# Attention in a decoder step: scores of head pairs in two double PSUM tiles, PE in source order

## The chip, the cores and the metric

The kernel runs on one core of a Trainium2 chip. The metric is the time of one execution on the device, in microseconds (us). The engines are called PE (TensorE, matmuls and transposes), DVE (VectorE), ACT (ScalarE), POOL (GpSimd) and SP (SyncE, which issues DMAs). PE writes its results into PSUM, eight banks of 512 f32 columns on 128 partitions.

## The reference

One inference step of a small hybrid decoder, width 1024, for a prompt of 256 tokens and 8 samples of one token each. Layer one is a state-space mixer (S5) and a squared-ReLU MLP; layer two is attention with three branches (compressed, selected and window keys), gated, and a second MLP. 16 query heads share 4 key and value heads of 64.

```python
kv = (_rms_norm(x, kv_norm) @ w_kv).reshape(nb, t, N_BRANCH, 2, N_KV_HEADS, HEAD_DIM)
# keys of the branches "selected" and "window": normed and rotated
k = _rope(_rms_norm(kv[:, :, br, 0], k_norm[br]), pos)
...
s_c = jnp.einsum('bqgrd,bngd->bqgrn', qg, kc)      # compressed: 8 blocks
p_c = _masked_softmax(s_c, ...)
s_s = ...; p_s = _masked_softmax(s_s, sel_mask)    # selected: here all 256 tokens
s_w = ...; p_w = _masked_softmax(s_w, w_mask)      # window: 256 tokens, causal
o = g[..., 0:1] * o_c + g[..., 1:2] * o_s + g[..., 2:3] * o_w
```

## The kernel before

All 264 tokens (8 samples, 256 prompt tokens) stand as columns, the width on the partitions. A dense layer takes 128x128 weight blocks; each weight is split into a high and a low part (`wh`, `wl`) and each block takes three matmuls of 264 columns (lines 597 to 599). The stages are S5, MLP, keys and values, queries and gates, attention, output projection, MLP. A scheduler of the language orders the instructions of each engine when the kernel is built; the source order is its input, and the pools of tiles (a tag has so many buffers) bind it, since a tile has to wait until its buffer is free.

Attention works on 12 units: two pairs of key heads (`gp`), two halves of the four query heads of each (`rp`), and for each the first 128 queries of two heads (`u` = 0) and then the last 128 of either (`u` = 1, 2). A unit has a step for the scores (`scores`), one for the softmax (`softmax`), one that turns the probabilities (`transposed`) and for `u` > 0 one that multiplies them with the values (`values`). The steps of three units run interleaved: scores of unit i, softmax of i-1, transposes and values of i-2. The two key heads of a pair (`g2`) lie in partitions 0 to 63 and 64 to 127; each has its own PSUM bank of scores, its own maximum, exponentials (with sums by ACT), reciprocal, gate and multiplication.

Around the units `side` calls two generators, `side_a` (the dense query tiles of the second head pair that are left, their norm and rotation in `q_post`, the compressed branch of the second half) and `side_b` (all of the samples' attention); tables say how many steps of each stand behind which unit:

```python
PSC = dict(fl=2, tr=3)
PSA = dict(mm=3)
PSB = dict(sc=2,po=1)
SIDE = (3,1,1,1,0,0,1,1,1,1,0,0,0,0)
SIDB = (1,2,2,2,2,2,2,2,0,0,0,0,0,0)
```

`PSC` are PSUM tags (banks each) that last the whole kernel, `PSA` those up to attention, `PSB` those from attention on. `kv_post` (lines 946 to 976) makes the keys ready: four transposes to token order (line 934, `token_major`), norm and rotation on ACT, DVE and POOL (`norm_rope`, lines 987 to 998), four transposes back (line 944, `feature_major`) and a copy into `KTp`, which the scores read. `q_post` does the same with two query heads, into `QT`. Two dense query tiles of the second pair stand ahead of attention (`Q1` = 2), two in `side_a`.

Of the kernel before, what the change touches and what calls it, by code (L numbers as in the profile page):

```python
# [157 lines left out]
def s5_stage(K, filler):  # L158
# [183 lines left out]
    def chunk_in(h):  # L342
# [3 lines left out]
        for q0 in range(0, 8, 3):  # L346
            n = min(3, 8 - q0)
            pt = [ps("mm"), ps("tr")]
# [177 lines left out]
    pys = {}  # L526
# [14 lines left out]
    for ft in range(4, 8):  # L541
        pys[ft] = ps("mm" if ft < 7 else "tr")
        conv(ft, pys[ft])
# [152 lines left out]
PDP = ()  # L696
PDA = ()
# [60 lines left out]
def sample_compress(K):  # L758
# [27 lines left out]
    for s in range(2):  # L786
# [3 lines left out]
        pts = [K.ps("fl"), K.ps("fl")]  # L790
# [157 lines left out]
def kv_post(K, br):  # L948
# [9 lines left out]
    pk = token_major(K, "sc", kv[:, 0:2])  # L958
# [6 lines left out]
    pv = token_major(K, "sc", kv[:, 2:4])  # L965
# [118 lines left out]
def gates(K, xh, xl):  # L1084
# [11 lines left out]
    S.activation(g, g, AF.Sigmoid)  # L1096
    K.gp = at.tile([128, 2, 16, 3], F32, name="gp")
# [44 lines left out]
def prompt_attn(K, oh, ol, side):  # L1142
# [6 lines left out]
    def cmp_branch(gp):  # L1149

        cS = aa.tile([128, 2, 8, 8], F32, tag="cS", name="cS", bufs=1)
        pcs = K.ps('po' if gp else PO)
# [22 lines left out]
        pt = K.ps('po' if gp else PO)  # L1175
# [3 lines left out]
        S.activation(pcts[gp], pt[0:64, 0:256], AF.Copy)  # L1179

    def scores(gp, rp, u):

        banks = [K.ps("sc"), K.ps("sc")]
# [16 lines left out]
        return banks  # L1200

    def softmax(gp, rp, u, banks):
        n = 4 if u == 0 else 2
        L = 512 // n
        out = []
        for g2 in range(2):
            head = (2 * gp + g2) * 4 + 2 * rp + max(u - 1, 0)
            sv = banks[g2].rearrange("p (n k) -> p n k", n=n)
            nm = aa.tile([128, n], F32, tag="nm", name="nm", bufs=6)
            den = aa.tile([128, n], F32, tag="den", name="den", bufs=6)  # L1210
# [5 lines left out]
            g = K.gp[:, 0, head:head + 2, 1:3] if u == 0 else K.gp[:, 1, head:head + 1, 1:3]  # L1216
            dv = den.rearrange("p (h b) -> p h b", b=2)
            V.tensor_tensor(dv, dv, g, ALU.mult)
            if (u > 0, g2) in PDA:
                for i in range(n):  # L1220
                    S.activation(P[:, i], P[:, i], AF.Copy, scale=den[:, i:i + 1])
            else:
                (G if (u > 0, g2) in PDP else V).tensor_tensor(P, P, den.unsqueeze(2).to_broadcast([128, n, L]), ALU.mult)
            out.append(P)
        return out

    def transposed(gp, rp, u, Ps, PTs):
        for g2 in range(2):
            pt = K.ps("tr")
            Pf = Ps[g2].rearrange("p n k -> p (n k)")  # L1230
# [29 lines left out]
    cmp_branch(0)  # L1260
    for i in range(n + 2):
        if i < n:
            sc[i] = scores(*units[i])
        if 1 <= i <= n:
            sm[i - 1] = softmax(*units[i - 1], sc.pop(i - 1))
        if i >= 2:
            gp, rp, u = units[i - 2]
            if u == 0:
                PTs = [aa.tile([128, 2, 2, 384], F32, tag="PT", name="PT", bufs=3) for _ in range(2)]
            transposed(gp, rp, u, sm.pop(i - 2), PTs)  # L1270
            if u > 0:
                values(gp, 2 * rp + u - 1, PTs[u - 1])
        side(i, cmp_branch)
# [17 lines left out]
def sample_qk(K):  # L1291
# [13 lines left out]
    if 1:  # L1305
        rsqrt_pool(nc, ak, ri, v, [128, 96])
    else:
        rsqrt_bits(nc, ak, ri, v, [128, 96])
    V.tensor_tensor(f(sq), f(K.sK), ri, ALU.mult)
# [14 lines left out]
    for gp in range(2):  # L1324
        for g2 in range(2):
            hs = slice(64 * g2, 64 * g2 + 64)
            c = 8 * gp + 4 * g2
            G.tensor_copy(K.Qbd[hs, :, gp, c:c + 4].rearrange("p b r -> p r b"), sR[hs, 4 + 4 * gp:8 + 4 * gp])

# [14 lines left out]
def sample_attn(K, oh, ol):  # L1344
# [6 lines left out]
    for bh in range(2):  # L1351
        p1, p2 = K.ps("mm"), K.ps("mm")
# [53 lines left out]
        pc = K.ps("mm")  # L1406
        nc.tensor.matmul(pc[:, 0:64], ptx[:, 0], K.vcs[:, bh], start=True, stop=True)
# [5 lines left out]
        V.tensor_tensor(o, o, pc[:, 0:64], ALU.add)  # L1413
# [34 lines left out]
def build(ctx, tc, A, O):  # L1448
# [13 lines left out]
    K.ps = lambda tag: pools[tag][0].tile([128, 512], F32, tag=pools[tag][2], name="ps_" + tag, bufs=pools[tag][1])  # L1462
# [63 lines left out]
    pools["mm"] = pools["fl"]  # L1526
    with ExitStack() as es:
# [59 lines left out]
        with ExitStack() as ek:  # L1587
            K.aa = ek.enter_context(tc.tile_pool(name="aa", bufs=1))

            def side_a(cmp_branch):  # L1590
                yield from q1
                for q in queue1:
                    yield from q
                cmp_branch(1)
                yield

            def side_b():
                sample_qk(K)
                yield
                yield from sample_attn(K, oh, ol)  # L1600
            steps = []

            def side(i, cmp_branch):
                if not steps:
                    steps.extend([side_a(cmp_branch), side_b()])
                for _ in range(SIDE[i]):
                    next(steps[0], None)
                for _ in range(SIDB[i]):
                    next(steps[1], None)
            prompt_attn(K, oh, ol, side)  # L1610
            for s in steps:
                for _ in s:
                    pass
        yh, yl = ft(F32R, "yh"), ft(F32R, "yl")
# [14 lines left out]
PSC = dict(fl=2, tr=3)  # L1629
PSA = dict(mm=3)  # L1630
PSB = dict(sc=2,po=1)
SIDE = (3,1,1,1,0,0,1,1,1,1,0,0,0,0)
SIDB = (1,2,2,2,2,2,2,2,0,0,0,0,0,0)
# [96 lines left out]
```

## Time and profile before

| | |
|---|---|
| median of 3 runs | 737.36 us (736.47 to 741.55) |
| the profiled execution | 741.12 us |
| its span, first to last instruction | 739.3 us |
| mean granted PE clock | 0.975 |
| PE busy | 700.2 us, 95% |
| DVE busy | 531.7 us, 72% |
| ACT busy | 404.6 us, 55% |
| POOL busy | 74.8 us, 10% |

The span is what the trace shows; the profiled execution's time has another 1.8 us around it. A mean granted clock of 1 would be PE at 2.4 GHz all the time. The attention stage, which the change is about, lies between some 435 and 528 us of the span.

### The profile page before, as it was taken

The numbers are of one execution on the slowest core, as the hardware profiler recorded it, in microseconds if no ns is written. First come the engines' busy times: TensorE is split into PE (matmuls) and PEld (weight loads), VectorE is DVE, ScalarE is ACT, GpSimd is POOL, SyncE is SP. The second block draws the span as 40 slices with busy tenths as digits, with TensorE's granted clock in tenths as the row PEclk, the third lists the DMA queues.
The fourth block names the chain that finished last, engine by engine and source line by source line (L and its number), as shares of the span: only waits on it lengthen the run. The fifth ranks groups of instructions, "written<-read, shape, count | busy, mean of one in ns | idle before, by whom it ended". The sixth has DMA issues, their size and how long they took to land.

```text
span 739.3 us, 16322 instructions
## 1 busy us (share of the span) xinstructions
PE 700.2 (95%) x6214; PEld 650.7 (88%) x6214; DVE 531.7 (72%) x1209; ACT 404.6 (55%) x907; POOL 74.8 (10%) x127
## 2 busy tenths in 40 slices
PE   2789897999999999999998999999999999999997
PEld 2787777999999999999988984565899999999997
DVE  7899995978777766656677868887678777755553
ACT  3463532666666655445466575657466666644442
POOL 0000623111000000000002224110020000000000
PEclk9989897999999999999999996999999999999999
DMA  7342423686767758555555564100255555556551
GB/s 263 81 158 77 161 99 118 197 289 193 229 234 262 277 175 298 186 175 188 177 175 179 188 187 142 59 3 1 86 172 182 188 173 182 189 180 201 192 190 40
DMA packets 53328, 124.70 MB, mean 169 GB/s; under 512 B 6522, under 2 KB 26874, under 8 KB 52994
## 3 DMA queue, kind: packets, MB, share of 16 engines
q1 hardware_dynamic: 51714, 121.23, 49.9%
q10 hardware_dynamic: 1536, 2.42, 0.9%
q8 instruction: 49, 0.80, 0.5%
q14 instruction: 29, 0.24, 0.1%
HBM read 120.63 MB, written 7.18 MB: 173 GB/s over the span
## 4 chain that ended last, share of the span: by engine, by line
PE 83%; DVE 13%; ACT 2%; issue 1%; DMA 1%; SPq 0%; ACTq 0%; DVEq 0%
PE ps_mm L597 23%; PE ps_mm L598 22%; PE ps_mm L599 22%; PE ps_sc L1195 3%; PE ps_tr L296 2%; PE ps_tr L1232 2%; PE ps_po L1253 2%; DVE ca L431 1%; DVE St L434 1%; DVE St L433 1%; DVE cb L432 1%; DVE St L455 1%; DMA U<-x_chunks_in 1%; DVE big L454 1%; PE ps_sc L1198 1%
## 5 line engine op out<-in xcount | busy, mean ns | idle before, releaser
L591 DVE TENSOR_TENSOR wl<-raw,wh 128x512 fp32r<-128x512 f32 x344 | 241.1, 703 | 149.5 <-ACT wh L590 146.5
L590 ACT ACTIVATE wh<-raw 128x512 fp32r<-128x512 f32 x344 | 216.0, 631 | 210.7 <-PE ps_mm L598 157.8
L597 PE MATMUL ps_mm<-hh,wh 128*128 128x264 f32 x512 | 145.3, 284 | 0.0
L598 PE MATMUL ps_mm<-hl,wh 128*128 128x264 f32 x512 | 145.0, 283 | 0.0
L599 PE MATMUL ps_mm<-hh,wl 128*128 128x264 f32 x512 | 145.0, 283 | 0.0
L598 PEld LDWEIGHTS ps_mm<-hl,wh 128*128 128x128 f32 x512 | 96.5, 188 | 0.0
L597 PEld LDWEIGHTS ps_mm<-hh,wh 128*128 128x128 f32 x512 | 96.4, 188 | 0.0
L599 PEld LDWEIGHTS ps_mm<-hh,wl 128*128 128x128 f32 x512 | 96.0, 187 | 0.0
L598 PE MATMUL ps_mm<-yl,wh 128*128 128x264 f32 x256 | 72.9, 285 | 0.0
L597 PE MATMUL ps_mm<-yh,wh 128*128 128x264 f32 x256 | 72.6, 284 | 0.0
L597 PE MATMUL ps_mm<-xh,wh 128*128 128x264 f32 x256 | 72.6, 284 | 0.0
L599 PE MATMUL ps_mm<-yh,wl 128*128 128x264 f32 x256 | 72.5, 283 | 0.0
L598 PE MATMUL ps_mm<-xl,wh 128*128 128x264 f32 x256 | 72.4, 283 | 0.0
L599 PE MATMUL ps_mm<-xh,wl 128*128 128x264 f32 x256 | 72.3, 284 | 0.0
L597 PEld LDWEIGHTS ps_mm<-yh,wh 128*128 128x128 f32 x256 | 48.2, 188 | 0.0
L598 PEld LDWEIGHTS ps_mm<-xl,wh 128*128 128x128 f32 x256 | 48.2, 188 | 0.0
L597 PEld LDWEIGHTS ps_mm<-xh,wh 128*128 128x128 f32 x256 | 48.2, 188 | 0.0
L599 PEld LDWEIGHTS ps_mm<-yh,wl 128*128 128x128 f32 x256 | 48.2, 188 | 0.0
L598 PEld LDWEIGHTS ps_mm<-yl,wh 128*128 128x128 f32 x256 | 48.1, 188 | 0.0
L599 PEld LDWEIGHTS ps_mm<-xh,wl 128*128 128x128 f32 x256 | 47.9, 188 | 0.0
L628 POOL TENSOR_TENSOR nacc<-nacc,sq 128x264 f32<-128x264 f32 x21 | 16.9, 803 | 251.9 <-ACT sq L627 251.9
L598 PE MATMUL ps_mm<-gl,wh 128*128 128x264 f32 x128 | 36.6, 289 | 0.0
(424 smaller groups left out, 1482.3 us busy)
## 6 DMA issues: line engine op xcount, KB each, us to landing
raw<-w_up_in SPq DMA_DIRECT2D x64, 512.0 KB, 3.8
raw<-w_down_in SPq DMA_DIRECT2D x64, 512.0 KB, 3.6
raw<-s_w_glu_in SPq DMA_DIRECT2D x16, 512.0 KB, 4.8
w<-cmp_w_in SPq DMA_DIRECT2D x12, 512.0 KB, 4.5
raw<-w_kv_in SPq DMA_DIRECT2D x12, 512.0 KB, 3.5
blk<-cache_cmp_in SPq DMA_DIRECT2D x64, 64.0 KB, 1.9
raw<-w_q_in SPq DMA_DIRECT2D x8, 512.0 KB, 3.7
win_old_out<-cache_win_kv_in SPq DMA_DIRECT2D x8, 510.0 KB, 5.2
```

Of the source, the lines that this page charges most:

```text
L296: nc.tensor.matmul(pm[:, 0:73], sameT, sq[:, h, q, b], start=(h + q + b == 0), stop=(h + q + b == 9))
L431: TT(a, x, m(SR), ALU.mult)
L432: TT(b_, x[:, ::-1], m(SQ), ALU.mult)
L590: nc.scalar.activation(h[:, :, cols], src[:, c:c + 4], AF.Copy)
L591: nc.vector.tensor_tensor(l[:, :, cols], src[:, c:c + 4], h[:, :, cols].bitcast(F32), ALU.subtract)
L597: nc.tensor.matmul(out, wh, xh, start=start, stop=False)
L598: nc.tensor.matmul(out, wh, xl, start=False, stop=False)
L599: nc.tensor.matmul(out, wl, xh, start=False, stop=stop)
L628: nc.gpsimd.tensor_tensor(self.acc, self.acc, sq, ALU.add)
L1195: nc.tensor.matmul(banks[g2], K.QT[hs[g2], 4 * gp + 2 * rp + u - 1, 128:256], K.KTp[hs[g2], gp], start=True, stop=False)
L1232: nc.tensor.transpose(pt[:, 128 * j:128 * j + 128], Pf[:, 128 * j:128 * j + 128], K.ident)
L1253: nc.tensor.matmul(po[64 * g2:64 * g2 + 64, 128 * kt:256], K.Vp[:, kt, br, 64 * g:64 * g + 64], rhs, start=False, stop=(br == 1 and kt == 1))
```

## The change

It has these parts. A tag `s2` of two tiles of two banks each takes the scores of a pair, and the two heads' score matmuls stand side by side. The softmax of a pair has one reduce, one reciprocal, one gate and one multiplication over 1024 columns; the exponentials stay one for each head and branch. PE is put in source order inside attention (`manual_schedule`), with a table that gives each step of side work a place between two units, ahead of the transposes (place 0) or behind them (place 1). Two dense query tiles are inside (`q` at units 0 and 1) and two ahead, as in the source before. Outside attention, dense work takes `fl` and the two `s2` tiles in turn; inside it takes `fl` alone. The keys' transposes move from `sc` to `tr`, which goes from three banks to two. `gates` loads the exponential's table early. `cmp_branch` and the samples' steps get yields, so that they can be cut.

```diff
     tm = K.ak.tile([128, 2, 512], F32, tag="tmk", name="tm", bufs=2)
-    pk = token_major(K, "sc", kv[:, 0:2])
+    pk = token_major(K, "tr", kv[:, 0:2])
...
     S.activation(g, g, AF.Sigmoid)
+    S.activation(ak.tile([1, 1], F32, name="tle"), g[0:1, 0:1], AF.Exp)
...
     def scores(gp, rp, u):

-        banks = [K.ps("sc"), K.ps("sc")]
+        pair = K.ps("s2")
+        banks = [pair[:, 0:512], pair[:, 512:1024]]
...
     def softmax(gp, rp, u, banks):
         n = 4 if u == 0 else 2
...
-        for g2 in range(2):
...
-            P = aa.tile([128, 522], F32, tag="P", name="P", bufs=4)[:, 0:512].rearrange("p (n k) -> p n k", n=n)
-            V.tensor_reduce(nm, sv, AX.X, ALU.max, negate=True)
-            for i in range(n):
-                S.activation(P[:, i], sv[:, i], AF.Exp, bias=nm[:, i:i + 1], accum_out=den[:, i:i + 1])
-            V.reciprocal(den, den)
...
+        sv = banks.rearrange("p (n k) -> p n k", n=2 * n)
...
+        P = aa.tile([128, 1024], F32, tag="P", name="P", bufs=2)
+        Pv = P.rearrange("p (n k) -> p n k", n=2 * n)
+        V.tensor_reduce(nm, sv, AX.X, ALU.max, negate=True)
+        for i in range(2 * n):
+            S.activation(Pv[:, i], sv[:, i], AF.Exp, bias=nm[:, i:i + 1], accum_out=den[:, i:i + 1])
+        V.reciprocal(den, den)
...
+        V.tensor_tensor(dv, dv, g, ALU.mult)
+        V.tensor_tensor(Pv, Pv, den.unsqueeze(2).to_broadcast([128, 2 * n, 512 // n]), ALU.mult)
+        return P[:, 0:512], P[:, 512:1024]
...
-    cmp_branch(0)
     for i in range(n + 2):
         if i < n:
             sc[i] = scores(*units[i])
         if 1 <= i <= n:
             sm[i - 1] = softmax(*units[i - 1], sc.pop(i - 1))
+        side(i, 0, cmp_branch)
         if i >= 2:
...
-        side(i, cmp_branch)
+        side(i, 1, cmp_branch)
...
-            prompt_attn(K, oh, ol, side)
-            for s in steps:
-                for _ in s:
+            K.mm = ["fl"]
+            with tc.manual_schedule(engines={nc.tensor.engine}):
+                prompt_attn(K, oh, ol, side)
+                for _ in steps["a"]:
                     pass
+            K.mm = list(wide)
...
-PSC = dict(fl=2, tr=3)
-PSA = dict(mm=3)
-PSB = dict(sc=2,po=1)
+PSC = dict(fl=1, tr=2)
+PSA = dict(mm=4, fb=1)
+PSB = dict(s2=2, po=1)
+SIDE = {(0, 0): "qc", (1, 0): "qc", (2, 0): "0", (3, 0): "0", (3, 1): "1s", (4, 1): "1", (5, 0): "s", (5, 1): "d",
...
```

Two places in PE's order. In such a row the line, the operation, output and inputs and their size stand, what it waits for, and how many like it follow one another (x4). Line numbers differ by a few between the two programs from the constants at 693 on: lines 932, 942, 1177, 1193, 1197, 1200 after are 934, 944, 1177, 1191, 1195, 1198 before.

The first is where the window keys, turned back (`tm`), come into the scores of unit 0. Before, on PE (`ps_mm`: the dense query tiles, which go on for another 20 rows until the scores L1191; the transposes of the same keys to token order stand 116 rows further up, most of the rows between dense):

```order
L597 MATMUL ps_mm<-qh,wh 128x264
L598 MATMUL ps_mm<-ql,wh 128x264
L599 MATMUL ps_mm<-qh,wl 128x264
L944 MATMUL ps_tr<-ident,tm 128x128 [waits Pool_49]
L944 MATMUL ps_tr<-ident,tm 128x128 x3
L1100 MATMUL ps_tr<-ident,gT 128x48 x2
L1108 MATMUL ps_tr<-cst,glt 128x3 [waits DVE_49,Activation_49]
L597 MATMUL ps_mm<-qh,wh 128x264
L598 MATMUL ps_mm<-ql,wh 128x264
L599 MATMUL ps_mm<-qh,wl 128x264
L1187 MATMUL ps_sc<-triR,identR 128x512
```

After, on PE, from those transposes (`kv`) to the scores (L1193) and the first dense row behind them:

```order
L932 MATMUL ps_tr<-ident,kv 128x128 [waits PE_49]
L932 MATMUL ps_tr<-ident,kv 128x128 x3
L1066 MATMUL ps_po<-ident,kcp 64x32 [waits DVE_49]
L1073 MATMUL ps_po<-vcp,cst 64x64 [waits PE_49,Activation_49]
L1073 MATMUL ps_po<-vcp,cst 64x64
L942 MATMUL ps_tr<-ident,tm 128x128 [waits Pool_49]
L942 MATMUL ps_tr<-ident,tm 128x128 x3
L932 MATMUL ps_tr<-ident,kv 128x128 x4
L1099 MATMUL ps_tr<-ident,gT 128x48 [waits Activation_49]
L1099 MATMUL ps_tr<-ident,gT 128x48
L1193 MATMUL ps_s_6037<-KTp,QT 128x256 x4
L597 MATMUL ps_fl<-qh,wh 128x264
```

The dense query tiles moved from between the two sets of transposes, and from ahead of the scores, to behind the scores.

The second is a query tile of the second half (`qr`, turned by L934 or L932), and the score matmuls of last queries. Before, on PE; the transposes back (L944 `qn`) follow 20 rows further down:

```order
L934 MATMUL ps_mm<-ident,qr_5939 128x128 [waits Activation_49]
L934 MATMUL ps_mm<-ident,qr_5939 128x128 x3
L1156 MATMUL ps_po<-kcb,QT 128x16 [waits DVE_49,PE_49]
L1156 MATMUL ps_po<-kcb,QT 128x16 x7
L1300 MATMUL ps_mm<-ssq,cst 128x96 [waits DMAHW4_49,DMAHW0_49,Activation_49]
L1195 MATMUL ps_sc<-KTp,QT 128x512 [waits DVE_49,Activation_49]
L1198 MATMUL ps_sc<-triR,identR 128x2x128
L1195 MATMUL ps_sc<-KTp,QT 128x512 [waits DVE_49,Activation_49]
L1198 MATMUL ps_sc<-triR,identR 128x2x128
L1195 MATMUL ps_sc<-KTp,QT 128x512 [waits DVE_49,Activation_49]
L1198 MATMUL ps_sc<-triR,identR 128x2x128
```

After, on PE, with the transposes of the compressed probabilities (`cS`) ahead, down to the transposes back (L942 `qn`):

```order
L1177 MATMUL ps_po<-ident,cS 64x128 [waits DMAHW3_49,DMAHW4_49,DVE_49,DMAHW7_49,PE_49,Pool_49]
L1177 MATMUL ps_po<-ident,cS 64x128
L1197 MATMUL ps_s_6165<-KTp,QT 128x512 [waits Activation_49]
L1197 MATMUL ps_s_6165<-KTp,QT 128x512
L1200 MATMUL ps_s_6165<-triR,identR 128x2x128 x2
L932 MATMUL ps_fl<-ident,qr_5941 128x128 [waits Activation_49]
L932 MATMUL ps_fl<-ident,qr_5941 128x128 x3
L1227 MATMUL ps_tr<-ident,P 128x128 x8
L1189 MATMUL ps_s_6229<-triR,identR 128x512 [waits PE_49]
L1189 MATMUL ps_s_6229<-triR,identR 128x512
L1193 MATMUL ps_s_6229<-KTp,QT 128x256 x4
L942 MATMUL ps_fl<-ident,qn 128x128 [waits Activation_49,Pool_49]
```

The two score matmuls became neighbours, and between the two sets of transposes of the query tile stand those of one unit (L1227) and the scores of one.

## Rows read from the trace of the kernel before

**Rows 1.** The page: busy us, share of the span and instructions by engine.

```profile
PE 700.2 (95%) x6214; PEld 650.7 (88%) x6214; DVE 531.7 (72%) x1209; ACT 404.6 (55%) x907; POOL 74.8 (10%) x127
```

**Rows 2.** Windows of the attention stage: length, busy us of each engine, clock, DMA share, GB/s.

```profile
core 0: us, PE busy (x) PEld busy (x) DVE busy (x) ACT busy (x) POOL busy (x), PEclk, DMA share, GB/s
441.00:446.00 5.00, 3.05 (x24) 2.66 (x23) 4.24 (x11) 4.83 (x16) 0.53 (x1) 1.00 0.88 257
446.00:460.00 14.00, 14.00 (x32) 6.91 (x31) 11.19 (x50) 7.15 (x28) 7.43 (x14) 0.51 0.42 136
...
500.00:521.00 21.00, 20.89 (x165) 11.84 (x157) 14.69 (x50) 12.86 (x56) 0.00 (x0) 1.00 0.00 1
```

**Rows 3.** Timeline of PE around its two waits: start, length us, operation, [idle before].

```profile
441.87 1.93 PE L1156 MATMUL ps_po<-kcb,QT 128*128 128x16 f32 x16 [0.35 <-DVE vcm L1079]
...
445.69 1.63 PE L1195 MATMUL ps_sc<-KTp,QT 64*128 64x512 f32 x2 [1.60 <-ACT P L1214]
...
447.75 2.07 PE L1195 MATMUL ps_sc<-KTp,QT 64*128 64x512 f32 x2
```

**Rows 4.** Timeline of PE: score matmuls of two row halves, together and one alone.

```profile
435.21 1.13 PE L1191 MATMUL ps_sc<-KTp,QT 64*128 64x256 f32 x8
...
476.31 1.13 PE L1191 MATMUL ps_sc<-KTp,QT 64*128 64x256 f32 x4
...
481.60 1.12 PE L1195 MATMUL ps_sc<-KTp,QT 64*128 64x512 f32 x2
```

**Rows 5.** Timelines of PE, DVE, POOL: the window keys, from transposes to transposes.

```profile
415.36 0.49 PE L934 MATMUL ps_sc<-ident,kv 128*128 128x128 f32 x3
...
417.52 0.67 DVE L988 TENSOR_REDUCE ss<-t 128x8 f32<-128x512 f32 x1
...
420.19 1.77 POOL L995 TENSOR_TENSOR tm<-tm,t 128x512 f32<-128x512 f32 x1 [2.62 <-ACT wh L590]
...
427.44 1.05 POOL L998 TENSOR_TENSOR tm<-tm,ri 128x512 f32<-128x512 f32 x1 [0.36 <-DVE ri L137]
...
430.65 0.60 PE L944 MATMUL ps_tr<-ident,tm 128*128 128x128 f32 x4
```

**Rows 6.** Timelines of ACT and DVE: the compressed keys and values handed on.

```profile
437.10 0.71 ACT L1070 ACTIVATE kcb<-ps_po 64x8 f32<-64x8 f32 x4 [1.31 <-PE ps_po L1068]
...
440.44 0.68 DVE L1079 TENSOR_TENSOR vcm<-ps_po,cst 64x512 f32<-64x512 f32 x1
```

**Rows 7.** Timelines of PE, ACT, POOL: a query tile of the second half, likewise.

```profile
474.66 0.60 PE L934 MATMUL ps_mm<-ident,qr 128*128 128x128 f32 x4
...
475.30 0.60 ACT L987 ACTIVATE t<-ps_mm 128x512 f32<-128x512 f32 x1 [0.18 <-PE ps_mm L934]
...
479.88 1.57 POOL L995 TENSOR_TENSOR qn<-qn,t 128x512 f32<-128x512 f32 x1 [12.62 <-ACT oh L606]
490.23 1.56 POOL L998 TENSOR_TENSOR qn<-qn,ri 128x512 f32<-128x512 f32 x1 [8.78 <-DVE den L1218]
...
491.84 0.66 PE L944 MATMUL ps_mm<-ident,qn 128*128 128x128 f32 x4
```

**Rows 8.** Timeline of ACT: exponentials of 256 and of 128 columns in a row.

```profile
474.08 0.49 ACT L1214 ACTIVATE P<-ps_sc,nm 128x256 f32<-128x256 f32 x1
...
474.53 0.49 ACT L1214 ACTIVATE P<-ps_sc,nm 128x256 f32<-128x256 f32 x1
...
479.64 0.36 ACT L1214 ACTIVATE P<-ps_sc,nm 128x128 f32<-128x128 f32 x1
...
479.99 0.37 ACT L1214 ACTIVATE P<-ps_sc,nm 128x128 f32<-128x128 f32 x1
```

**Rows 9.** Groups by shape, 441 to 530 us: count, busy us, mean ns, idle before.

```profile
L1223 DVE TENSOR_TENSOR P<-P,den 128x512 f32<-128x512 f32 x24 | 16.6, 691 | 0.4
...
L133 DVE TENSOR_TENSOR rs<-rs 128x8 f32<-128x8 f32 x6 | 1.3, 215 | 0.0
...
L606 ACT ACTIVATE oh<-ps_po 128x256 fp32r<-128x256 f32 x8 | 3.1, 384 | 10.4 <-PE ps_po L1253 10.0 <-PE ps_mm L1357 0.4
```

More of the change, by code (lines that the diff above doesn't have):

```diff
@@ L541, in s5_stage @@
     for ft in range(4, 8):
-        pys[ft] = ps("mm" if ft < 7 else "tr")
+        pys[ft] = ps("mm")
         conv(ft, pys[ft])
@@ L695 @@
 NP = 'm'
-PDP = ()
-PDA = ()
 CPA = (0,)
@@ L1151, in cmp_branch @@
         cS = aa.tile([128, 2, 8, 8], F32, tag="cS", name="cS", bufs=1)
-        pcs = K.ps('po' if gp else PO)
+        pcs = K.ps(PO)
         for qt in range(2):
@@ L1174, in cmp_branch @@
         V.tensor_tensor(cS, cS, dn.unsqueeze(3).to_broadcast([128, 2, 8, 8]), ALU.mult)
-        pt = K.ps('po' if gp else PO)
+        yield
+        pt = K.ps(PO)
         for qt in range(2):
@@ L1199, in scores @@
                                  K.triR.unsqueeze(1).to_broadcast([128, 2, 128]), start=False, stop=True)
-        return banks
+        return pair
     def softmax(gp, rp, u, banks):
         n = 4 if u == 0 else 2
-        L = 512 // n
-        out = []
-        for g2 in range(2):
[L1207 to L1210, printed above, removed]
-            P = aa.tile([128, 522], F32, tag="P", name="P", bufs=4)[:, 0:512].rearrange("p (n k) -> p n k", n=n)
-            V.tensor_reduce(nm, sv, AX.X, ALU.max, negate=True)
-            for i in range(n):
-                S.activation(P[:, i], sv[:, i], AF.Exp, bias=nm[:, i:i + 1], accum_out=den[:, i:i + 1])
-            V.reciprocal(den, den)
[L1216 to L1224, printed above, removed]
@@ L1351, in sample_attn @@
     for bh in range(2):
-        p1, p2 = K.ps("mm"), K.ps("mm")
+        pair = K.ps("s2")
+        p1, p2 = pair[:, 0:512], pair[:, 512:1024]
         for pp, o, n in ((p1, 0, 265), (p2, 265, 257)):
@@ L1405, in sample_attn @@
                                      vr[bh][br][:, b4, pg], start=False, stop=(br == 1 and pg == 1))
-        pc = K.ps("mm")
-        nc.tensor.matmul(pc[:, 0:64], ptx[:, 0], K.vcs[:, bh], start=True, stop=True)
+        pc = po[:, 256:320]
+        nc.tensor.matmul(pc, ptx[:, 0], K.vcs[:, bh], start=True, stop=True)
         t = K.tmp.tile([128, NT], F32, tag="t", name="so")[:, 0:256].rearrange("p (g d) -> p g d", g=4)
@@ L1412, in sample_attn @@
         V.tensor_reduce(o, t.rearrange("p g d -> p d g"), AX.X, ALU.add)
-        V.tensor_tensor(o, o, pc[:, 0:64], ALU.add)
+        V.tensor_tensor(o, o, pc, ALU.add)
         yield
@@ L1461, in psum, with ps @@
             pools[tag] = pool, bufs[tag], tag
-    K.ps = lambda tag: pools[tag][0].tile([128, 512], F32, tag=pools[tag][2], name="ps_" + tag, bufs=pools[tag][1])
+    K.mm = ["mm"]
+    def ps(tag):
+        if tag == "mm":
+            tag = K.mm[0]
+            K.mm.append(K.mm.pop(0))
+            if tag == "s2":
+                return ps(tag)[:, 0:512]
+        pool, bufs, t = pools[tag]
+        return pool.tile([128, 1024 if tag == "s2" else 512], F32, tag=t, name="ps_" + tag, bufs=bufs)
+    K.ps = ps
     psum(ctx, "pc", PSC)
@@ L1525, in build @@
     psum(ctx, "pa", PSB)
-    pools["mm"] = pools["fl"]
+    wide = ["fl", "s2", "s2"]
+    K.mm = list(wide)
     with ExitStack() as es:
@@ L1588, in build, with side @@
             K.aa = ek.enter_context(tc.tile_pool(name="aa", bufs=1))
[L1590 to L1609, printed above, removed]
-            prompt_attn(K, oh, ol, side)
-            for s in steps:
-                for _ in s:
+            steps = {"q": q1, "s": sample_qk(K), "a": sample_attn(K, oh, ol)}
+            def side(i, place, cmp_branch):
+                steps.setdefault("c", cmp_branch(0))
+                steps.setdefault("d", cmp_branch(1))
+                for x in SIDE.get((i, place), ""):
+                    next(steps[x] if x not in "01" else queue1[int(x)], None)
+            K.mm = ["fl"]
+            with tc.manual_schedule(engines={nc.tensor.engine}):
+                prompt_attn(K, oh, ol, side)
+                for _ in steps["a"]:
                     pass
+            K.mm = list(wide)
         yh, yl = ft(F32R, "yh"), ft(F32R, "yl")
```

21 lines of the change are left out of this document (14 added, 7 removed).

## The prediction

> **What bounds the kernel now.** The page comes first [rows 1]: PE is busy 700.2 of 739.3 us, DVE 531.7, ACT 404.6. So a microsecond that the change takes off DVE or ACT pays only where PE waits for it, and a wait that it puts before PE is paid in full. The windows of the attention stage say where PE waits today [rows 2]: 3.05 us of work in the five from 441 on, then no idle time worth naming up to 521 (14.00 of 14.00, and 20.89 of 21.00 at the end). The timeline names the two waits in the gap [rows 3]: 0.35 us for the masked compressed values, 1.60 us for a score bank that the first exponentials still hold. The third thing to see is the clock: the granted clock is 0.51 between 446 and 460, the lower of the two levels (1.2 of 2.4 GHz), right behind that gap, and 1.00 before and after. A 512-wide score matmul takes 2.07 us there [rows 3] and 1.12 later [rows 4]. The other engines wait for PE today, not PE for them: before the eight output splits ACT idles 10.0 us for PE's values [rows 9].
>
> The profiled execution took 741.12 us, 3.8 above the median of 737.36. I make the sum on the profiled one and take 3.8 off at the end.
>
> **What it can give.** Three terms.
>
> Scores in pairs. The heads of a pair lie in the two halves of PE's rows. Four 256-wide matmuls in both halves, issued in a row, take 1.13 us; the two of one bank alone take 1.13 as well [rows 4]. So neighbours in different halves run at the same time. Before, a 512-wide matmul (1.12 us) stands alone, with its mask and often transposes before its partner; after, the partners are neighbours. If the 512-wide ones overlap as the 256-wide do, each of 8 units saves 1.12 less a few hundredths for the start of the second, say 1.05: 8.4 us. Two of the four units of the first kind are split too (476.31 and its like): 2 x 1.05 = 2.1. Together 10.5; the lower bound is 2.1, if the wider ones don't overlap.
>
> The Trainium skill, "TensorEngine Tiling (Array Packing)", says that different row tiles must write different PSUM banks. The pair tile spans two banks, one for each head, so by that rule the 10.5 stands.
>
> The clock. At half clock 13.6 of the 14 us do 6.8 us of full-clock work. If nothing idles before it, 6.8 come back; the bound is 0.
>
> The waits of 0.35 and 1.60, with the table load that now sits in the gates: 2.0.
>
> DVE has half as many reduces, reciprocals and multiplications for the scores. A 512-wide one takes 0.69 [rows 9]; twice the width lies between 0.69 and 1.38 and I take 1.2, so 12 of each save some 4 us of DVE. None of it is PE's by itself, since PE waits for DVE nowhere between 446 and 521. ACT's exponentials are as many as before. The other tile sets before attention (one bank for side work, four for the dense work) move a few instructions under PE work that stays; I take 0, bounds -2 and +2.
>
> Gains: 10.5 + 6.8 + 2.0 = 19.3 us.
>
> **What it costs.** PE now runs the attention code in source order. What stands between a transpose and the matmul that needs its result is then fixed by hand, and where it is less than the chain, PE waits. For each such place I added the chain from rows and took off the PE work inside it; hand-overs between engines are counted at 0.2 each (0.18 in ACT's row of [rows 7]).
>
> First scores. The window keys were transposed at 415.36 and came back to PE at 430.65 [rows 5]: 15 us, all under dense matmuls. After, the transposes stand directly before the first scores, with small transposes alone between; the dense tiles that covered them stand behind those scores. The chain: square on ACT 0.6 (as at 475.30, rows 7), reduce, two products and scales on DVE 2.4 (0.67 for the first, rows 5), handing on the compressed keys 0.2 + 0.71 on ACT and the compressed values 1.28 on DVE, which is in DVE's order ahead of the end of the square root [rows 6], two small PE steps between, some 0.6 together (four transposes take 0.60, rows 7), the last four steps of the root 0.8 (0.2 each, rows 9), the multiplication on POOL 1.05, four transposes 0.45 and the copy 0.6, nine hand-overs 1.8, small transposes that share the two banks 1.5: 12.4, with 1.8 of PE work inside. **10.6.** Bounds: 8 (the root doesn't wait for the compressed values), 13 (the 15 us it took before, less the 1.8).
>
> Compressed probabilities of the first half. Their transposes stand ahead of the third scores. On DVE their normalising is queued behind the multiplication of the first pair, and that behind eight exponentials, 0.35 apart [rows 8]. **2.4**; bounds 0 and 4.
>
> First query tile of the second half. Before it took 17 us from 474.66 to 491.84 [rows 7], with thirty rows between. After, its two halves have eight transposes and one set of scores between them, 2.6 us. The chain: 0.6 on ACT, 2.4 on DVE (POOL's addition, 1.57, runs beside the root), six steps of the root 1.2, then in DVE's order the reduce of the scores just made (1.2) and the multiplication of the pair before (1.2 with 0.8 for its small ones), three more steps 0.6, POOL 1.3 to 1.56, hand-overs 0.6: 9.6 to 10. **7.0**; bounds 5 and 14 (17 less the 2.6).
>
> Second such tile, the same chain behind the eight exponentials of a unit and the output split: **4.7** where the sample's first small matmul stands ahead of it, and **2.6** at the sample's rotation, which is POOL's and DVE's. Bounds 3 and 14.
>
> Compressed probabilities of the second half: **3.9**, queued on DVE behind the reduce of the next pair. Bounds 1 and 6.
>
> The eighth scores, which wait for the exponentials of the unit two before, eight of 0.35 behind the sample's: **2.2**. Bounds 0 and 4.
>
> The rest: transposes of a unit and its values now stand together, with 0.6 us of PE work between a transpose and the copy that the values read (0.6 on ACT or DVE and two hand-overs), and two sample outputs wait for DVE's reduce: ten waits of 0.1 to 2.6, together **8.4**. Before, such neighbours had other units' scores between. Bounds 3 and 12.
>
> Losses: 10.6 + 2.4 + 7.0 + 4.7 + 2.6 + 3.9 + 2.2 + 8.4 = 41.8 us. Net 41.8 - 19.3 = 22.5 slower: 741.1 + 22.5 - 3.8 = 759.8. The bounds of the losses add up to 20 and 67, but DVE and ACT catch up in one wait what makes the next, so I don't expect both ends; I take 759.
>
> **The rivals.**
>
> The order holds (faster). PE waits at the first scores alone, and the engines have caught up in those 10.6 us, so that every later chain runs free: the two query tiles at their bare 0.6 + 2.4 + 2.2 + 1.3 less the work between are then some 3 us each, of which DVE's short queue takes another part. Losses 10.6 - 2.6 (its lower bound) = 8, and nothing else: 741.1 + 8 - 19.3 - 3.8 = 726. It decides if the waits add up to less than 12 us. For it: DVE loses 24 long instructions of 0.69 and gets 12 of 1.2. Against: the chains of rows 5 and 7 are latencies, not load, and no engine's idle time shortens them. 0.13.
>
> They cancel (no change, within 1%, about what a measurement of this kernel can tell from no change). The losses stay near their lower bounds, 20, and the gains are whole: 738. 0.15.
>
> The clock falls again. The lower level came in this trace after five microseconds with 3.05 busy [rows 2, 3]; the change makes at least one gap twice as long, and some shorter ones close together. Then the 6.8 is not won, and a second stretch of that length costs another 6.8: 759 + 6.8 to 759 + 13.6, 766 to 773; four of them 786. The Trainium skill, "TensorE: Matmul & The Clock Gate", section "A second HAM failure mode: psum-queue depth-cycling", speaks for this one: a kernel that cycles through PSUM banks with PE briefly idle between groups of matmuls sees its clock go up and down again. No row of the kernel before shows such a cycle, only the one fall. 0.25.
>
> The change doesn't do what it says: the 512-wide pairs run one after the other. 8.4 us of gain are gone, but a busier PE hides some 2.5 of the waits: 759 + 6 = 765. It lies inside the range; 0.1 within the forecast's own share.
>
> **How the numbers follow.** My forecast (745 to 766) has 0.47, the clock 0.25, no change 0.15, faster 0.13. Slower by over 1%: 0.47 + 0.25 = 0.72. The range leaves out most of the faster rival and four or more falls of the clock: 736 to 784.
>
> **What would show it.** In the profile after: no 512-wide score matmul alone, and two of them in about 1.2 us; PE idle for some 10 us before the first scores, released by ACT's copy of the keys or POOL's multiplication; 7 us before the second transposes of a query tile, released by POOL; sums of PE's idle time of 35 to 45 us between the first scores and the output projection; the clock low for at least one stretch. The forecast is wrong if the keys' transposes come earlier against the dense matmuls than the order of PE lets me see, if PE's idle time in the stage is under 20 us, or if time goes in the stages before attention, which I put at nothing.

## The result and the profile after

The changed kernel takes 766.04 us (762.80 to 770.64, 4 runs) against 739.45 (736.47 to 741.92, 4 runs) for the kernel before: 1.0366 times as long, 95% interval 1.0286 to 1.0446. The profiled execution took 763.48 us, its span is 761.7, its mean granted clock 0.966. The page, against [rows 1]:

```profile
PE 694.9 (91%) x6214; PEld 651.6 (86%) x6214; DVE 528.8 (69%) x1161; ACT 403.0 (53%) x908; POOL 70.1 (9%) x127
...
PEclk9979899999999999999999878999999999999999
```

PE is busy 5.3 us less and the span is 22.4 us longer: PE waits. The windows of the attention stage (length, busy us of each engine, clock, DMA share, GB/s), against [rows 2]:

```profile
core 0: us, PE busy (x) PEld busy (x) DVE busy (x) ACT busy (x) POOL busy (x), PEclk, DMA share, GB/s
425.00:445.00 20.00, 10.09 (x68) 8.47 (x69) 11.57 (x48) 8.94 (x22) 4.21 (x5) 0.71 0.12 40
445.00:470.00 25.00, 16.43 (x111) 12.84 (x107) 18.14 (x45) 12.48 (x48) 2.90 (x4) 0.91 0.28 96
470.00:500.00 30.00, 21.16 (x128) 14.04 (x132) 18.12 (x52) 12.22 (x45) 10.19 (x27) 0.84 0.20 63
500.00:530.00 30.00, 26.57 (x231) 15.96 (x224) 18.69 (x44) 18.01 (x80) 0.00 (x0) 0.97 0.24 72
530.00:560.00 30.00, 27.54 (x225) 21.90 (x226) 16.73 (x41) 14.53 (x46) 0.38 (x1) 1.00 0.13 42
```

In 75 us from 425 on PE works 47.7 (before, it had no idle time worth naming after 446), and the clock is between 0.71 and 0.91 in them. The waits of PE in the stage (us in total, times, longest):

```profile
engine line waited for: us in total, times, longest us
PE ps_fl L942 <- POOL qn L996: 7.0, 1, 7.0
PE ps_po L1066 <- DVE kcp L753: 4.0, 1, 4.0
PE ps_fl L1295 <- DVE rs L128: 4.0, 1, 4.0
PE ps_po L1177 <- DVE cS L1173: 3.7, 1, 3.7
PE ps_tr L942 <- POOL tm L996: 3.6, 1, 3.6
PE ps_fl L1414 <- DVE so L1411: 3.3, 2, 2.4
PE ps_po L1177 <- issue: 2.3, 1, 2.3
...
PE ps_tr L942 <- POOL qn L996: 1.3, 1, 1.3
```

These are the places of the prediction, one by one. At the first scores: 1.3 + 4.0 + 0.8 + 3.6 = 9.7 us, in this order for a query tile of the first pair on POOL (`qn`), the compressed keys (L1066, L1073) and the window keys on POOL (`tm`). Before the first query tile's transposes back: 7.0, for POOL. At the sample's first small matmul (L1295): 4.0. It writes the dense bank `ps_fl`, which the second query tile's norm reads until this row of DVE's timeline; the matmul starts at 480.69:

```profile
479.79 0.75 DVE L991 TENSOR_TENSOR t<-ps_fl,T1q 128x256 f32<-128x256 f32 x2
```

At the compressed probabilities: 2.3 and 3.7. PE's timeline shows the pair:

```profile
487.92 1.13 PE L1197 MATMUL ps_s<-KTp,QT 64*128 64x512 f32 x4
488.98 0.51 PE L1200 MATMUL ps_s<-triR,identR 128*128 128x256 f32 x2
```

Four records of 512 columns (two of each head) take 1.13 us, as two did before [rows 4]: the neighbours run at the same time. DVE's groups by shape (count, busy, mean ns, idle before) price the wide instructions, against 691 ns in [rows 9]:

```profile
L1219 DVE TENSOR_TENSOR P<-P,den 128x1024 f32<-128x1024 f32 x12 | 14.6, 1220 | 0.3
L1211 DVE TENSOR_REDUCE nm<-ps_s 128x4 f32<-128x1024 f32 x8 | 9.7, 1215 | 1.1 <-PE ps_s L1200 0.9
```

To compare the runs I take the stage from the first dense matmul of the keys (`kh`) to the first of the second MLP (`yh`), and split it for PE: gaps of over 0.1 us between its records (idle); half of the time that it is busy at the lower clock (what the clock costs); the rest is its work at full clock. The entries are good to 0.1. The idle time that the expectations below give for the changed kernel (33 us) leaves out 2.9 of it, two waits ahead of attention.

| kernel | ratio to before (95%) | stage us | idle | clock costs | work |
|---|---|---|---|---|---|
| before | 1 | 190.0 | 4.7 | 6.9 | 178.5 |
| changed | 1.0366 (1.0286 to 1.0446) | 214.7 | 36.1 | 10.2 | 168.5 |
| PE left to the scheduler | 1.0084 (1.0036 to 1.0132) | 196.8 | 19.2 | 6.9 | 170.8 |
| one transposes step later | 1.0259 (1.0161 to 1.0357) | 213.2 | 29.8 | 14.4 | 169.0 |
| four query tiles ahead | 1.0558 (1.0466 to 1.0650) | 230.9 | 39.3 | 23.1 | 168.5 |
| pairs taken apart | 1.0540 (1.0432 to 1.0649) | 230.2 | 31.7 | 21.5 | 177.1 |
| window keys first | 1.0330 (1.0252 to 1.0408) | 213.9 | 29.4 | 16.2 | 168.3 |
| waits filled with dummies | 1.0417 (1.0344 to 1.0490) | 216.5 | 27.0 | 10.2 | 179.3 |
| scheduler, softmax in halves | 1.0071 (0.9989 to 1.0153) | 194.8 | 16.9 | 7.8 | 170.2 |
| source order, wider table | 1.0266 (1.0170 to 1.0361) | 209.4 | 26.0 | 15.8 | 167.6 |
| scheduler, four single banks | 1.0223 (1.0119 to 1.0326) | 208.2 | 10.4 | 17.0 | 180.8 |
| source order, table moved again | 1.0157 (1.0040 to 1.0273) | 201.8 | 21.9 | 11.0 | 168.9 |
| scheduler, halves, keys first | 1.0036 (0.9985 to 1.0088) | 194.2 | 14.8 | 10.7 | 168.7 |
| the same with the wider table | 1.0007 (0.9958 to 1.0057) | 190.6 | 12.7 | 8.3 | 169.6 |

What stands ahead of the stage (354.8 to 363.9 us) varies from execution to execution, and what stands behind it takes 190 us in all of them; neither goes with the change. So the stage's 24.7 us are the loss: 31.4 more idle, 3.3 more for the clock, 10.0 less work.

The split is of one execution of each kernel, and executions of the same kernel differ in their granted clock. The profiled one of the changed kernel has the highest of its four (0.966; the others 0.964, 0.958 and 0.955, with times up to 770.64), so the 3.3 is probably the low end of what the clock takes there. A difference in the clock column says something about an edit only where the other executions bear it out. They do for four tiles ahead (0.943 to 0.947 in all four) and pairs taken apart (0.941 to 0.952) against the changed kernel (0.955 to 0.966), and for four single banks (0.955 to 0.963) against the scheduler with halves (0.968 to 0.977). They don't for one transposes step later, window keys first and source order with the wider table, whose mean clocks (0.964, 0.959 and 0.961) lie within 0.004 of the changed kernel's 0.961.

### The profile page after: what moved, and what is told of

The parts are those of the page before. It is cut to its first block, busy times and chain, and to the rows that moved or that the text cites. A ratio compares the mean times of both kernels' runs of the same rounds, so it can differ in the third digit from the quotient of the medians.

```text
span 761.7 us, 16256 instructions
## 1 busy us (share of the span) xinstructions
PE 694.9 (91%) x6214; PEld 651.6 (86%) x6214; DVE 528.8 (69%) x1161; ACT 403.0 (53%) x908; POOL 70.1 (9%) x127
## 4 chain that ended last, share of the span: by engine, by line
PE 76%; DVE 14%; ACT 5%; issue 2%; DMA 1%; POOL 1%; SPq 0%; ACTq 0%; DVEq 0%; POOLq 0%
PE ps_mm L598 10%; PE ps_mm L597 10%; PE ps_mm L599 10%; PE ps_s L598 8%; PE ps_s L597 8%; PE ps_s L599 8%; PE ps_fl L597 4%; PE ps_fl L598 4%; PE ps_fl L599 4%; ACT P L1213 2%; PE ps_tr L296 2%; DVE P L1219 1%; PE ps_fl L793 1%; PE ps_fb L793 1%; PE ps_po L1248 1%
## 5 line engine op out<-in xcount | busy, mean ns | idle before, releaser
L597 PE MATMUL ps_mm<-hh,wh 128*128 128x264 f32 x256 | 72.6, 284 | 0.0
L598 PE MATMUL ps_mm<-hl,wh 128*128 128x264 f32 x256 | 72.5, 283 | 0.0
L599 PE MATMUL ps_mm<-hh,wl 128*128 128x264 f32 x256 | 72.5, 283 | 0.0
L597 PE MATMUL ps_s<-hh,wh 128*128 128x264 f32 x192 | 54.5, 284 | 0.0
L598 PE MATMUL ps_s<-hl,wh 128*128 128x264 f32 x192 | 54.4, 283 | 0.0
L599 PE MATMUL ps_s<-hh,wl 128*128 128x264 f32 x192 | 54.4, 283 | 0.0
L598 PEld LDWEIGHTS ps_mm<-hl,wh 128*128 128x128 f32 x256 | 48.2, 188 | 0.0
L597 PEld LDWEIGHTS ps_mm<-hh,wh 128*128 128x128 f32 x256 | 48.2, 188 | 0.0
L599 PEld LDWEIGHTS ps_mm<-hh,wl 128*128 128x128 f32 x256 | 48.0, 187 | 0.0
L597 PE MATMUL ps_s<-yh,wh 128*128 128x264 f32 x168 | 47.7, 284 | 0.0
L628 POOL TENSOR_TENSOR nacc<-nacc,sq 128x264 f32<-128x264 f32 x21 | 16.2, 773 | 255.7 <-ACT sq L627 255.6
```

The source lines that it names most:

```text
L597: nc.tensor.matmul(out, wh, xh, start=start, stop=False)
L598: nc.tensor.matmul(out, wh, xl, start=False, stop=False)
L599: nc.tensor.matmul(out, wl, xh, start=False, stop=stop)
L628: nc.gpsimd.tensor_tensor(self.acc, self.acc, sq, ALU.add)
```

## Experiments

The theory: PE's fixed order leaves chains of other engines uncovered, and the neighbouring pairs pay back some 10 us. The rivals: what costs is the bank layout with the wide softmax; or it is the clock.

**PE left to the scheduler.** All else as changed.

```diff
-            with tc.manual_schedule(engines={nc.tensor.engine}):
+            if True:
                 prompt_attn(K, oh, ol, side)
```

> The changed kernel with PE in attention left to the scheduler again (all else as changed: pair tiles, single softmax instructions, banks, table of side work). Theory (fixed order of PE leaves the chains uncovered): PE's idle time in the stage falls from 33 us to under 10, the dense query tiles lie between the two sets of key transposes again, time 733 to 745 us. Rival (the bank layout and the wide softmax cost it: one dense bank, two transpose banks, two buffers of probabilities): idle stays over 25 us, 758 to 768.

749.21 us, stage 196.8: 17.9 of the 24.7 us are gone, 16.9 of them idle. Its largest waits:

```profile
PE ps_s L1197 <- ACT P L1213: 3.8, 2, 3.5
PE ps_fl L1309 <- DVE ssq L1307: 2.4, 1, 2.4
...
PE ps_fl L942 <- DVE sv L1297: 1.6, 1, 1.6
```

The 7.0, the 4.0 and 3.6 for the keys, and both waits for compressed probabilities are no more; the largest that is left is for a score tile that the first exponentials hold. The theory holds for most of the loss, though not for all: idle is 19.2, not under 10, and the time lies above the range. The share of the wide softmax and of the score tiles is what later runs ask; the other banks (one for dense work, two for transposes) weren't varied in any run.

**One transposes step later.** One entry of the table.

```diff
-SIDE = {(0, 0): "qc", (1, 0): "qc", (2, 0): "0", (3, 0): "0", (3, 1): "1s", (4, 1): "1", ...
+SIDE = {(0, 0): "qc", (1, 0): "qc", (2, 0): "0", (3, 1): "1s", (4, 0): "0", (4, 1): "1", ...
```

> The changed kernel with one entry of the table moved: the transposes back of the first query tile of the second half stand one unit later. Theory (the wait is the chain less the PE work inside): the 7.0 us wait before them goes to under 1.5; the chain of the second tile now ends nearer, so its waits (4.0 and 0.35) grow by 1 to 3; net -3 to -6 us, 760 to 763. Rival (POOL or DVE is too slow at this place whatever PE's order): the wait moves along with the transposes and stays over 5 us, time as the changed kernel.

761.50 us, as forecast, though its interval overlaps the changed kernel's. The largest waits:

```profile
PE ps_fl L1295 <- DVE rs L128: 4.6, 1, 4.6
PE ps_po L1066 <- DVE kcp L753: 4.0, 1, 4.0
PE ps_po L1177 <- DVE cS L1173: 3.7, 1, 3.7
PE ps_tr L942 <- POOL tm L996: 3.6, 1, 3.6
```

The wait of 7.0 is gone and hasn't moved along, so it was the place, not POOL. The next one grew by 0.6, and a new one of 1.1 came before values; idle fell by 6.3. In the profiled execution the stage gained only 1.5, as the clock took 4.2 of it (10.2 to 14.4) and work 0.5. That isn't the edit's doing as far as the runs show: the profiled execution is the slowest of its four (764.20), and their mean clock is no lower than the changed kernel's (0.964 against 0.961).

**Four query tiles ahead.** The two dense tiles inside attention go to the front.

```diff
-SIDE = {(0, 0): "qc", (1, 0): "qc", ...
+SIDE = {(0, 0): "c", (1, 0): "c", ...
-Q1 = 2
+Q1 = 4
```

> The changed kernel with all four dense query tiles of the second pair ahead of attention instead of two inside. Theory: the scheduler puts them between the two sets of key transposes, the 9.7 us idle before the first scores (4.0 + 0.8 + 3.6 + 1.3) falls under 2.5; 5.8 us of cover are then missing behind the first scores, so that new waits of 3 to 6 us come before the compressed probabilities' or the first probabilities' transposes; net -3 to -6 us, 759 to 763. Rival (the cover isn't what is missing): the idle before the first scores stays over 7 us.

782.54 us, which neither the theory nor the rival had. The two largest waits in PE's timeline, and the window that holds them:

```profile
448.10 1.11 PE L942 MATMUL ps_tr<-ident,tm 128*128 128x128 f32 x4 [5.79 <-POOL tm L996]
...
469.31 0.61 PE L1177 MATMUL ps_po<-ident,cS 128*64 128x128 f32 x2 [9.41 <-issue]
```

```profile
445.00:470.00 25.00, 12.49 (x50) 9.17 (x50) 9.39 (x27) 7.38 (x33) 1.65 (x2) 0.50 0.16 58
```

The scheduler did put the dense tiles between the keys' transposes, and the idle time there fell from 9.7 to 6.6, not under 2.5: 5.8 us of cover against a chain that the prediction put at 12 and that took 11.2 in the changed kernel (from the end of the keys' transposes, 432.41, to the first scores, 443.65). Then 9.4 us open where the tiles had stood, before the compressed probabilities. The clock is 0.50 all through the window and costs 23.1 us in the stage, 12.9 more than in the changed kernel. With the dense tiles gone from attention, more went to the clock than to waits; I had priced only the waits.

**Pairs taken apart.** Each score matmul followed by its own mask.

```diff
             for g2 in range(2):
                 nc.tensor.matmul(banks[g2], K.QT[hs[g2], 4 * gp + 2 * rp + u - 1, 128:256],
                                  K.KTp[hs[g2], gp], start=True, stop=False)
-            for g2 in range(2):
                 nc.tensor.matmul(banks[g2].rearrange("p (b k) -> p b k", b=2)[:, :, 128:256], K.identR,
```

> The changed kernel with each 512-wide score matmul followed at once by its own mask, so that the partners in the two row halves are no neighbours. Theory (neighbours overlap): a pair with its masks takes 1.05 us more, 8.4 us of PE work in 8 units, of which 2 to 4 lie in waits that exist already: +4 to +7 us, 770 to 773. Rival (512-wide ones don't overlap): no difference in PE's busy time, time as the changed kernel.

781.76 us, above the range. The score matmuls as a group, in the changed kernel and here, and two windows of this run:

```profile
L1197 PE MATMUL ps_s<-KTp,QT 64*128 64x512 f32 x32 | 9.8, 690 | 0.0
```

```profile
L1197 PE MATMUL ps_s<-KTp,QT 64*128 64x512 f32 x32 | 20.9, 739 | 0.0
```

```profile
445.00:470.00 25.00, 22.09 (x101) 16.59 (x101) 10.87 (x28) 10.77 (x39) 2.36 (x3) 0.70 0.21 67
470.00:500.00 30.00, 19.77 (x80) 13.00 (x81) 18.15 (x50) 10.84 (x41) 8.72 (x16) 0.67 0.27 87
```

Busy time of the group doubles, work rises by 8.6 us (8.4 forecast) and idle falls by 4.4, as the theory has it. The time rose by more than it allows, because the clock costs 11.3 more. That taking the pairs apart brings the lower clock is shown by this edit (all four executions lie below all four of the changed kernel); by which mechanism isn't.

**Window keys first.** One constant.

```diff
-KVQ = 0
+KVQ = 1
```

> The changed kernel with the window keys' dense tiles ahead of the first queries' (one constant), so that the keys' chain has the four dense query tiles of the first pair to run under; the first query tile's transposes now stand 46 dense matmuls (5.6 us) ahead of its transposes back. Theory (a chain of 10 to 12 us less the PE work put inside it): of the 9.7 us idle before the first scores some 4 to 5 are left (10 less 5.6, now for the queries), the rest of the stage as in the changed kernel; -4 to -8 us, 757 to 762. Rival (the first scores wait for something else than the keys): idle there stays over 8 us, time as the changed kernel.

764.35 us, above the range. Of the 9.7 us idle before the first scores 4.8 are left, as forecast, but not for the queries: they are the 4.0 and 0.8 of the compressed keys, which stayed as they were, a chain of its own that I had not priced apart. (The queries' came behind the scores, 1.2 and 0.7.) Idle in the stage fell by 6.7. In the profiled execution the clock took 6.0 of it; over the four executions the mean clock is 0.959 against 0.961 and the interval overlaps the changed kernel's, so what the edit is worth in time stays open.

**Waits filled with dummies.** Six places of the table's waits (the expectation counts seven), 88 transposes of the identity in all.

```diff
+def fill(K, out, n):
+
+    for _ in range(n):
+        K.nc.tensor.transpose(out, K.ident, K.ident)
...
         pt = K.ps(PO)
+        fill(K, pt[:, 256:384], 24 if gp else 12)
```

> The changed kernel with dummy transposes of the identity put on PE in seven of its waits (4 to 24 of about 0.11 us, into parts of the banks that the real results don't use or overwrite), no wait taken away. Theory that part of the loss is the clock, which falls behind the waits: the low clock between 425 and 560 us, 27 us in the changed kernel, falls under 17, and the time by half of what is gone, 3 to 6 us, to 760 to 763. Rival (the clock is only a sign of the waits): low clock about as long, time the same or up to 3 us more.

771.35 us. Idle fell by 9.1, work rose by 10.8, and the clock costs 10.2 as before. One window:

```profile
470.00:500.00 30.00, 22.68 (x136) 15.80 (x132) 19.71 (x58) 10.76 (x43) 8.81 (x16) 0.77 0.24 76
```

The rival's: dummy transposes in these gaps don't keep the clock up here. The run doesn't settle whether idle time brings the lower clock, since 27.0 us of it are left: the 9.7 before the first scores had no dummies, and the lower stretch of 13.7 us that begins there stayed as it was. Where the dummies stand, the lower clock fills 13.7 us (478.2 to 491.9), as it filled 13.6 in three stretches of the changed kernel.

**Scheduler, softmax in halves.** The pair tiles stay; two instructions of 512 columns for each of 1024.

```diff
-        V.tensor_reduce(nm, sv, AX.X, ALU.max, negate=True)
+        for g2 in range(2):
+            sv = banks[:, 512 * g2:512 * g2 + 512].rearrange("p (n k) -> p n k", n=n)
...
+            V.tensor_reduce(nm, sv, AX.X, ALU.max, negate=True)
```

> The kernel with PE left to the scheduler (749 us) and the softmax in two halves of 512 columns again, in the same pair tiles. Theory (single instructions save DVE time that PE doesn't wait for, and start the first exponentials 0.5 us later): within 3 us of 749 either way. Rival A (the wide instructions are what lengthens the waits for exponentials): idle in the stage from 16 to under 10 us, 741 to 744. Rival B (they are what pays): over 755.

746.68 us, stage 194.8 against 196.8: the wide instructions neither pay nor cost much, and the two intervals overlap. The largest waits:

```profile
PE ps_s L1197 <- ACT P L1216: 5.6, 3, 3.9
PE ps_fl L942 <- POOL qn L996: 2.2, 1, 2.2
```

Scores still wait 5.6 us for exponentials.

**Scheduler, four single banks.** The same with four tiles of one bank for the scores.

```diff
-PSB = dict(s2=2, po=1)
+PSB = dict(sc=4, po=1)
...
-        pair = K.ps("s2")
-        banks = [pair[:, 0:512], pair[:, 512:1024]]
+        banks = [K.ps("sc"), K.ps("sc")]
```

> The kernel with PE left to the scheduler and the softmax in halves (747 us), with four one-bank score tiles in place of two double ones, so that a bank comes free after its own head's exponentials; the scheduler then puts the two heads' score matmuls apart again. Theory (neighbours in the two row halves are the change's gain, some 8 us; the double tile makes scores wait for both heads' exponentials, 5.6 us in the run before): PE's busy time in the stage 7 to 8 us up, its waits for exponentials down by 3 to 5, 748 to 753. Rival (the double tile is what costs in this version): 738 to 744.

758.74 us, above the range, on the theory's side. The waits for exponentials fell to 1.5 and idle to 10.4, while the pairs came apart and work rose by 10.6. The rest is the clock, in these windows:

```profile
455.00:460.00 5.00, 2.74 (x9) 1.19 (x9) 5.00 (x15) 4.54 (x24) 0.00 (x0) 1.00 0.65 203
460.00:484.00 24.00, 24.00 (x69) 13.18 (x67) 16.53 (x59) 10.21 (x43) 7.25 (x14) 0.50 0.08 25
```

**Source order, wider table.** Keys first, and the table with its steps further apart.

```diff
-SIDE = {(0, 0): "qc", (1, 0): "qc", (2, 0): "0", (3, 0): "0", (3, 1): "1s", (4, 1): "1", (5, 0): "s", (5, 1): "d",
-        (6, 0): "da", (6, 1): "a", (7, 1): "a", ...
+SIDE = {(0, 0): "qc", (0, 1): "q", (1, 0): "0", (2, 0): "c", (2, 1): "1", (3, 0): "s", (3, 1): "0", (4, 1): "1", (5, 0): "sd",
+        (6, 0): "a", (6, 1): "da", (7, 1): "a", ...
```

> The changed kernel with the window keys' dense tiles first and another table of side work, PE still in source order: a query tile's transposes back stand two units or more behind its transposes, the compressed probabilities' one unit later, the samples' rotation two units behind their squares. Theory (source order costs only where too little stands inside a chain): PE's idle time in the stage from 33 to 10 to 16 us, with less low clock, 741 to 750. Rival (source order itself, or the layout, costs it): idle over 25 us, over 757.

759.36 us, idle 26.0: by these numbers the rival's. The largest waits:

```profile
PE ps_po L1177 <- issue: 4.4, 1, 4.4
PE ps_fl L1295 <- DVE rs L128: 4.2, 1, 4.2
PE ps_po L1066 <- DVE kcp L753: 4.0, 1, 4.0
```

The two query tiles' waits are gone, but the compressed probabilities, one unit later, wait longer (4.4 for 2.3), and the sample's small matmul (L1295) waits 4.2, as it did in the changed kernel; in both it takes the single dense bank next after the second query tile's transposes. The next run moves these.

**Source order, table moved again.**

```diff
-... (2, 0): "c", (2, 1): "1", (3, 0): "s", (3, 1): "0", (4, 1): "1", (5, 0): "sd", (6, 0): "a", (6, 1): "da", (7, 1): "a",
+... (2, 1): "c1", (3, 1): "0s", (4, 1): "1", (5, 0): "d", (5, 1): "s", (6, 1): "a", (7, 1): "da",
-        (11, 0): "a", (11, 1): "a", (12, 0): "a"}
+        (11, 0): "a", (11, 1): "a", (12, 1): "a"}
```

> The version in source order with the window keys first and the wider-spaced table (759 us), with six entries of the table moved once more: the compressed probabilities' transposes behind a unit's, the samples' squares behind the first query tile's transposes back, the last sample output one place later. Theory (each wait is a chain less the work put inside it): of the five waits of 2.4 to 4.4 us at the moved places (18 us) 8 to 12 go, the 4.0 before the compressed keys and 2.5 before the first query tile stay; 747 to 753. Rival (the waits only move to the next place): idle within 4 us of the version before, 756 to 762.

754.01 us, 1 above the theory's range: idle 4.1 less, where the rival had up to 4, and the clock 4.8 less. Behind the transposes back, the sample's matmul waits 0.7 in place of 4.2: its wait was for the dense bank. But the compressed probabilities still wait 3.6 of their 4.4, and a new wait of 2.6 came (L1155). This step by itself isn't clear of the noise (1.0157 against 1.0266, the intervals overlap). Both steps together are: 1.0157 against the changed kernel's 1.0366, both in source order, so over half of the loss lay in the places.

**Scheduler, halves, keys first; and the same with the wider table.** The constant and the last table, put into the version with PE left to the scheduler and the softmax in halves.

> The version with PE left to the scheduler and the softmax in halves (746.7 us, stage 194.8) with the window keys' dense tiles first. Theory: its waits ahead of the first scores, 1.4 + 0.9 + 0.7 + 0.5 us, go for the most part, the 3.9 for the first exponentials and later ones stay: 740 to 746, about equal to the kernel before. Rival (the scheduler had hidden the keys already, and the queries' shorter chain costs as much): 746 to 750.

> The same with the wider-spaced table of side work as the scheduler's input. Theory (the scheduler finds the places itself, the table is only its order among equals): within 3 us of the version without it. Rival (the table decides as much as under source order): 5 us or more apart.

741.59 and 741.57 us: both as forecast, and neither distinguishable from the kernel before (1.0036 and 1.0007). No version that I ran beats it. They keep the pairs' 9 to 10 us of work and give them to 8 to 10 us more of idle time and 1.4 to 3.8 for the clock.

## Why the prediction was right, point by point

Its time was 759, its range 736 to 784, its likeliest case 745 to 766; the measured 766.04 lies where that case ends and the rival "the clock falls again" (766 to 773) begins. That the total came out near is in part luck: two of its terms were off by 8 and 10 us, in opposite directions.

- **What it can give, scores in pairs**, 10.5: right. Work fell by 10.0, and taking the pairs apart put 8.6 back where 8.4 was counted for the wide ones. The place where it rests on the Trainium skill, "TensorEngine Tiling (Array Packing)", section "Gotcha 1: PSUM Pressure" (row tiles write different PSUM banks), agrees with the trace: 1.13 us for both, in the two banks of a tile.
- **The clock**, 6.8 to come back: this step failed. It costs 10.2 in the stage where it cost 6.9, so 3.3 were lost and the term is off by 10. The rival "the clock falls again" had this, at 0.25: the lower clock came at 389.1, 433.5, 467.6, 481.3 and 498.4 us. The first of these, 3.4 us long, lies ahead of attention, where the prediction put nothing; it is 1.7 of the 3.3. The Trainium skill, "TensorE: Matmul & The Clock Gate", section "A second HAM failure mode: psum-queue depth-cycling", has a clock that goes up and down behind brief idle times of PE. The ups and downs are in the trace; that the idle times bring them, no run here shows by itself, and filling some of them with dummies didn't help.
- **What it costs**, 41.8 less the 2.0 of before: idle rose by 31.4. Counted from the first scores on, the waits are 33 us, just under the 35 to 45 that the prediction named as a sign. The mechanism was right and the sum 8.4 too large; the clock's 10.1 went the other way, and so the total of 22.5 came out near the 24.7 measured.
- Place by place, forecast and measured: first scores 10.6, 9.7; compressed probabilities 2.4, 2.3 and 3.9, 3.7; first query tile 7.0, 7.0; second tile and samples 4.7, 4.0 (for the dense bank, so for the first half of the tile's chain alone, up to DVE's last read of it) and 2.6, 0.35. The mis-sized ones are small: the sample's rotation, the eighth scores (2.2; no such wait is in the trace) and "the rest" (8.4; the listed others are 3.3 for the sample outputs, 1.6 and 0.9, 5.8 together).
- **First scores**: the terms listed add up to 12.0, not to the 12.4 that stands there, so that the sum should have given 10.2. The chain took 11.2, and 8.4 of the 9.7 us of waits lie in it. The prediction named the keys alone as what PE waits for. The run with the keys first shows a second chain beside it, that of the compressed keys, which holds PE for 4.0 whatever the keys do.
- DVE's wide instruction, 1.2 taken: 1.22. That none of the saving is PE's: with PE left to the scheduler, the version in halves was 2.0 us shorter in the stage, not longer.
- **The order holds**, the faster rival, needed waits under 12 us; the best version in source order still has 21.9 idle.

Still open: why the lower clock comes in some stretches of this stage and not in others, and with that how the 10 to 20 us that it costs in the worst versions could be had back. One of them isn't chance: the stretch of 3.4 us between 389 and 400, ahead of attention, stands in the traces of all eight changed versions that have the window keys second, and in none of the five with the window keys first, nor in the kernel before. Open too is what the single dense bank and the two transpose banks cost: the best versions with PE left to the scheduler have them, and idle 8 to 10 us more than the kernel before.

## What to carry to other kernels

When an engine's order is fixed by hand, list each pair of instructions of it between which a chain of other engines runs, and hold the chain's length (from the trace) against the work put between; do it for every chain at a place, since the second one stays when the first is covered. Two matmuls in different halves of PE's rows took the time of one here when they were neighbours (1.13 us for both), and a tile that holds both kept them so, at the price of a later release (5.6 us of waits for exponentials against 1.5). Dense work that fills waits may be keeping the clock as well: moving it away cost 12.9 us of clock here and 3.2 of idle time.

## What the hardware showed unasked

The granted clock is 0.50 from 460 to 484 us in the version with four single banks while PE is busy 24.00 of 24.00 us; in the five before it had worked 2.74. So the lower clock outlasted its gap with no idle time in it. PE's timeline there:

```profile
469.58 2.07 PE L1196 MATMUL ps_sc<-KTp,QT 64*128 64x512 f32 x2
471.58 0.58 PE L1199 MATMUL ps_sc<-triR,identR 128*128 128x256 f32 x1
...
475.76 1.05 PE L1227 MATMUL ps_tr<-ident,P 128*128 128x128 f32 x4
...
481.26 2.78 PE L1248 MATMUL ps_po<-PT,Vp 128*64 128x256 f32 x16
...
484.55 1.12 PE L1196 MATMUL ps_sc<-KTp,QT 64*128 64x512 f32 x2
```

Score matmuls in one half of the rows (L1196), masks and transposes fill the stretch; the clock rose when a set of values (L1248) had run. What of this kept it low wasn't tried.

And 88 dummy transposes left the clock's cost at 10.2 us, though PE was idle 9.1 less.
